# Hybrid gMLP and attention decoder step: two token tiles of v take the places of two gate tiles between the last attention blocks

## The chip, the cores and the metric

The kernel runs on one core of one Trainium2 chip. The metric is the device time of one execution in microseconds. The core's engines are TensorE (PE, with its weight loads listed apart as PEld), VectorE (DVE), ScalarE (ACT), GpSimd (POOL) and SyncE (SP), whose queue issues nearly all DMAs.

## The reference

One post-norm decoder layer is applied to 512 prompt tokens and 64 sample tokens (8 requests of 8 tokens), with the same weights and a width of 1024. All is in float32:

```python
h = x @ w_in                      # columns: gMLP u | gMLP v | q | k | attention v | gate_A | gate_B
u  = gelu(h[..., O_U:O_V])
va = layer_norm(gelu(h[..., O_V:O_Q]), ln_v_g, ln_v_b)
g_a, g_b = sigmoid(gate_A columns), sigmoid(gate_B columns)
y_a = u * (tril(W_s) applied to va in chunks of 128 positions + b_s)
y_b = sliding-window attention with sinks (window 128, 16 heads, 4 key/value heads)
m   = (g_a * (y_a @ w_pa) + g_b * (y_b @ w_pb)) @ w_o
x   = layer_norm(ALPHA * x + m);  x = layer_norm(ALPHA * x + swiglu(x))
```

The outputs are the new x of both groups, the key and value windows, and the normalised v rows of the sample tokens.

## The kernel before

A float32 product is made from three products of the fast format: each operand is split into a rounded part (hi, written by ACT) and the remainder (lo, written by DVE); hi by hi, hi by lo and lo by hi are summed in PSUM. Weights come as a stream of units of 128 x 1024 numbers (`wall`), in the order in which `_weights` puts them: `fetch` (L120) loads a unit into one of three `raw` buffers, and `convert` (L130) splits it into one of four `hi` and four `lo` buffers. `unit` (L145) hands out the next unit and splits `ahead` further ones.

There are three ways to multiply. `fm` (L302) makes a column tile of 128 output columns for all 576 tokens: 48 matmuls of 288 columns, weights stationary. `tm` (L315) makes a token tile: 128 tokens by 512 output columns, tokens stationary, 24 matmuls of 512 columns for a prompt tile over the 8 parts of the contraction (16 for the sample tile). `pair` (L218) makes two column tiles at once by the seven-product scheme of Strassen and Winograd: 7 products of 12 matmuls of 288 columns. It needs sums of quarters of x (`XSums`, and a fourth sum written over X), sums of quarters of the weights (`weight_group`, L158, on DVE and POOL) and additions of the results on DVE.

The work around the change stands in this order:

- **Attention.** There are 16 blocks (4 key/value heads by 4 windows). Between the steps of a block TensorE makes one column tile of w_in, listed in `FILLS` (L71): q and k tiles still missing, the eight u tiles, and last, in blocks 14 and 15 (counted from 0), the gate tiles g0 and g1 of g_a.
- **v** (`gmlp`, L876). The first 512 columns of v (here v0) are made for five token tiles at once, four units after each other; beside it run the sample tokens' attention values and, for four chunks, the loads and sums of quarters of x (`input_loads`, `input_sum`: 2 DMAs, 2 operations of POOL, 5 of DVE and 3 of ACT a chunk). Then come gelu of u and the second 512 columns (v1): three token tiles one by one, the last two together. `evacuate` applies gelu, `norm_steps` the layer norm on DVE.
- **Gates** (`merge`, L1019). Seven pairs make the other 14 gate tiles. Spare work (the rest of the norms, the eight `spatial_gate` steps, splits of y_a) is dealt out at fixed spots of the pairs. In this stage the order is the program's; in the two stages before a planner orders each engine's instructions, save where `issue_after` binds one behind another.
- Then the products with w_pa, w_pb and w_o, and the feed-forward part, whose pairs have the same seven products.

In the profile the gate tiles of the attention are called psg, the u tiles psu, v's sums acc_v, a pair's three sums x, y and z (xg for the gates, xf for the feed-forward part), attention's values po, the transposes of the samples' probabilities pst, the chunks xr, their split sums XS1h and so on, and weights ghi/glo in pairs, hi/lo elsewhere.

Of the kernel before, what the change touches and what calls it, by code (L numbers as in the profile page):

```python
# [70 lines left out]
FILLS = [tuple(x) for x in "q3 u0 k1 q4 q5 u1 q6 q7 u2 u3 u4 u5 u6 u7 g0 g1".split()]  # L71
# [8 lines left out]
class Builder:  # L80
# [678 lines left out]
    def projections_and_attention(self):  # L759
# [6 lines left out]
        self.kt, self.qs, self.u, self.T = [], {}, [], []  # L766
# [25 lines left out]
        for i, (g, n) in enumerate(blocks):  # L792
# [18 lines left out]
            fill = self.column_tile(*fills[i], ahead=1 + before_last)  # L811
# [18 lines left out]

    def column_tile(self, kind, c, ahead=1):

        ps = self.PS(f"ps{kind}{c}")
        u = self.unit(KC, ahead=ahead)
        self.fm(ps, u, self.xact, ks=range(7))
        yield
        self.fm(ps, u, self.xact, ks=range(7, KC))
        yield
        if kind == "k":
            self.evac_k(ps, c)  # L840
        elif kind == "q":
            self.evac_q(ps, c)
        else:
            tiles = self.u if kind == "u" else self.T
            if c % 2 == 0:
                tiles.append(self.C([2, NT], F32, f"{kind}{c}"))
            self.copied = self.nc.scalar.copy(
                out=tiles[c // 2][:, c % 2].rearrange("p (b c) -> p b c", b=2), in_=ps[:, :, :HB])
# [27 lines left out]
    def gmlp(self):  # L876
# [26 lines left out]
        def tile(t, out, u, ks):  # L903
            for k in ks:
                wh, wl = u[k // 2]
                self.tm(out, (*self.xact(k), self.XS[:, k, :]), wh[:, k % 2], wl[:, k % 2], t, k == 0, k == KC - 1)

        def evacuate(t, acc, half):
            s = slice(512 * half, 512 * half + 512)
            if t < NB:  # L910
                nc.scalar.activation(out=v[t][:, s], in_=acc, func=AF.Gelu_apprx_tanh)
            else:
                low = self.SG(f"vlow{half}")
                nc.scalar.copy(out=low[:NS, :512], in_=acc[NS:])
                self.low_added = nc.vector.tensor_tensor(
                    out=low[:NS, :512], in0=acc[:NS], in1=low[:NS, :512], op=ALU.add)
                nc.scalar.activation(out=v[t][:NS, s], in_=low[:NS, :512], func=AF.Gelu_apprx_tanh)
# [4 lines left out]
        acc = self.accumulators("v0")  # L922
        for n in range(4):
            with self.tc.issue_after(self.copied.ins):
                u = {n: self.unit(2)}
            for t in range(NB + 1):
                tile(t, acc[t], u, (2 * n, 2 * n + 1))
            if n == 0:
                self.sample_rest()
            if n == 1:  # L930
                self.input_sums()
                for c in range(3):
                    self.input_sum(c)
                fourth = self.input_loads(3)
        for t in range(NB + 1):
            evacuate(t, acc[t], 0)
        with self.tc.issue_after(self.turned.ins):
            for t in self.u:
                nc.scalar.activation(out=t[:], in_=t[:], func=AF.Gelu_apprx_tanh)
        us = [self.unit(2, ahead=int(n < 3)) for n in range(4)]  # L940
        for t in range(3):
            acc = self.bank(f"acc_v1_{t}")
            tile(t, acc, us, range(KC))
            if t == 0:
                with self.tc.issue_after(self.last_split.ins):
                    self.input_sum(3, fourth)
# [72 lines left out]
    def merge(self):  # L1019
        nc = self.nc  # L1020
        for t in self.T:
            nc.scalar.activation(out=t[:], in_=t[:], func=AF.Sigmoid)
        left = self.left(self.X, (*self.XSums[:2], self.input_sum3(), self.XSums[2]))
        self.first_pair(self.low_added)
        T = [self.T[0][:, i] for i in range(2)]
        gB = []
# [20 lines left out]
        with self.tc.manual_schedule():  # L1047
            for i in range(7):
                if i in (3, 4):
# [361 lines left out]
def _weights(w_in, w_pa, w_pb, w_o, w_gate, w_up, w_down):  # L1411
# [22 lines left out]
    start = {"q": o_q, "k": o_k, "u": 0, "g": o_g}  # L1434
    for kind, c in FILLS:
        fm(col(start[kind], c))
    for i in range(2):
        tm(w_in[:, o_v + 512 * i : o_v + 512 * i + 512])
    for j in range(2, 16, 2):
# [85 lines left out]
```

## Time and profile before

| | us |
|---|---|
| median of 3 runs | 877.47 |
| lowest of them | 877.05 |
| profiled execution, own time | 876.51 |
| span of the profiled execution | 874.8 |
| PE busy in the span | 864.8 |
| DVE, ACT, POOL busy | 629.4, 405.5, 194.5 |

The span runs from the first to the last instruction; the execution's own time is 1.7 us longer. The third of the three runs took 1218.6 us and stands far from the other two. All stage times below are in us from the span's start.

### The profile page before, as it was taken

How to read it: one execution, taken by the hardware profiler on the slowest of the kernel's cores; microseconds unless marked ns; L12 is line 12 of the kernel's file. 1: busy time of each engine (PE TensorE's matmuls, PEld its weight loads, DVE VectorE, ACT ScalarE, POOL GpSimd, SP SyncE). 2: the span in 40 equal slices, each digit the busy share in tenths (PEclk: the TensorE clock that was granted, in tenths of full speed). 3: DMA queues.
4: the chain of work that ended last, by engine and by line, in shares of the span. 5: the costliest groups of instructions: out<-in, count | busy, mean ns of one | idle time of the engine just before them, and what ended most of it. 6: DMA issues, size and time to landing. Idle time of an engine off the chain costs nothing.

```text
span 874.8 us, 14728 instructions
## 1 busy us (share of the span) xinstructions
PE 864.8 (99%) x5907; PEld 816.8 (93%) x5907; DVE 629.4 (72%) x933; ACT 405.5 (46%) x770; POOL 194.5 (22%) x206
## 2 busy tenths in 40 slices
PE   9999999999999999999999999999999999999996
PEld 7999999988899999999888999999999998888885
DVE  5878897657898888767778767777777789124237
ACT  6566566575464464333423544444444557111110
POOL 2013324253242203133203122222222210000003
PEclk9999999999999999999999999999999999999999
DMA  8422124255123134324640032222222335222202
GB/s 304 156 100 62 61 73 148 61 175 163 47 100 102 63 121 142 118 98 157 217 144 0 13 101 91 92 93 91 90 90 95 95 105 188 94 75 95 73 1 108
DMA packets 31168, 91.85 MB, mean 105 GB/s; under 512 B 3963, under 2 KB 9244, under 8 KB 31068
## 3 DMA queue, kind: packets, MB, share of 16 engines
q1 hardware_dynamic: 30764, 88.64, 30.9%
q10 hardware_dynamic: 336, 2.28, 0.7%
q8 instruction: 46, 0.75, 0.4%
q14 instruction: 22, 0.18, 0.1%
HBM read 86.77 MB, written 6.10 MB: 106 GB/s over the span
## 4 chain that ended last, share of the span: by engine, by line
PE 94%; DVE 3%; ACT 1%; DMA 0%; issue 0%; POOL 0%; DVEq 0%; SPq 0%; POOLq 0%; ACTq 0%
PE d L300 16%; PE xf L300 15%; PE zf L300 7%; PE acc_v L300 6%; PE acc_o L300 6%; PE pspa L300 6%; PE xg L300 5%; PE psu L300 5%; PE yf L300 4%; PE psq L300 4%; PE ffn L300 3%; PE xp L300 3%; PE zg L300 3%; PE psav L300 2%; PE psg L300 1%; PE zp L300 1%
## 5 line engine op out<-in xcount | busy, mean ns | idle before, releaser
L118 DVE TENSOR_TENSOR lo<-raw,hi 128x1024 fp32r<-128x1024 f32 x70 | 87.5, 1255 | 94.0 <-ACT hi L117 93.7
L118 DVE TENSOR_TENSOR glo<-raw,ghi 128x1024 fp32r<-128x1024 f32 (+1 forms) x93 | 100.5, 1087 | 53.6 <-ACT ghi L117 53.6
L300 PE MATMUL d<-hi,h 128*128 128x512 f32 (+1 forms) x440 | 128.0, 368 | 0.0
L117 ACT CAST hi<-raw 128x1024 fp32r<-128x1024 f32 x70 | 72.7, 1049 | 103.2 <-PE d L300 82.6
L117 ACT CAST ghi<-raw 128x1024 fp32r<-128x1024 f32 (+1 forms) x93 | 83.4, 900 | 58.7 <-DVE raw L180 56.9
L300 PEld LDWEIGHTS d<-hi,h 128*128 128x128 f32 x440 | 79.9, 189 | 13.8
L300 PE MATMUL d<-lo,h 128*128 128x512 f32 (+1 forms) x242 | 89.6, 370 | 0.0
L180 POOL TENSOR_TENSOR raw<-raw,t 128x512 f32<-128x512 f32 x31 | 41.0, 1323 | 193.3 <-DVE glo L118 164.1
L180 POOL TENSOR_TENSOR t<-raw,raw 128x512 f32<-128x512 f32 x31 | 43.0, 1387 | 111.9 <-DVE raw L180 111.9
L300 PE MATMUL xf<-x1T,ghi 128*128 128x288 f32 x320 | 64.9, 295 | 0.0
L118 DVE TENSOR_TENSOR glo<-t,ghi 128x1024 fp32r<-128x1024 f32 x31 | 63.0, 2032 | 1.9 <-ACT ghi L117 1.9
L300 PEld LDWEIGHTS d<-lo,h 128*128 128x128 f32 x242 | 45.6, 189 | 7.8
L300 PEld LDWEIGHTS xf<-x1T,ghi 128*128 128x128 f32 x320 | 51.3, 188 | 0.3 <-DVE u L231 0.2
L330 POOL TENSOR_SCALAR lnr<-lnmv 128x1 f32<-128x1 f32 (+1 forms) x15 | 12.3, 818 | 169.8 <-DVE lnmv L348 166.5
L645 POOL TENSOR_SCALAR_AFFINE_SELECT pc<-pt 128x512 fp32r<-128x512 f32 x24 | 23.1, 963 | 110.8 <-ACT pt L117 102.7
L300 PE MATMUL xf<-x1T,glo 128*128 128x288 f32 x160 | 47.1, 294 | 0.0
L300 PE MATMUL acc_o<-hi,m 128*128 128x512 f32 x144 | 46.4, 391 | 0.0
L621 ACT ACTIVATE work<-work,att 128x128 f32<-128x128 f32 x64 | 25.0, 392 | 42.1 <-DVE att L618 37.5
L300 PE MATMUL pspa<-yA,hi 128*128 128x288 f32 x256 | 44.3, 294 | 0.0
L300 PE MATMUL psu<-X,hi 128*128 128x288 f32 x256 | 44.1, 294 | 0.0
L300 PE MATMUL acc_v<-hi,X 128*128 128x512 f32 x128 | 41.8, 391 | 0.0
L300 PE MATMUL psq<-X,hi 128*128 128x288 f32 x224 | 38.8, 294 | 0.3 <-DVE kt L513 0.3
(370 smaller groups left out, 2472.6 us busy)
## 6 DMA issues: line engine op xcount, KB each, us to landing
raw<-in_wall_dram SPq DMA_DIRECT2D x132, 512.0 KB
open<-in_open_dram SPq DMA_DIRECT2D x7, 416.0 KB
xr<-in_xT_dram SPq DMA_DIRECT2D x8, 288.0 KB
z<-in_xtok_dram SPq DMA_DIRECT2D x4, 512.0 KB
out_y_prompt_dram<-z SPq DMA_DIRECT2D x3, 512.0 KB
circ<-bout SPq DMA_DIRECT2D x1, 1024.0 KB
Bsel<-circ SPq DMA_DIRECT2D x2, 512.0 KB
kc<-in_kcT_dram SPq DMA_DIRECT2D x2, 512.0 KB
```

The source lines that it names most:

```text
L117: self.nc.scalar.copy(out=hi, in_=src)
L118: return self.nc.vector.tensor_tensor(out=lo, in0=src, in1=hi.bitcast(F32), op=ALU.subtract)
L180: sub = lambda e, out, x, y: e.tensor_tensor(out=out, in0=x, in1=y, op=ALU.subtract)
L300: self.last_mm = self.nc.tensor.matmul(out, l, r, start=start, stop=stop, **more)
L330: self.nc.gpsimd.tensor_scalar_add(r[:n], mv[:n, 1:2], EPS)
L621: nc.scalar.activation(out=pr[:, r], in_=sel[:, r], func=AF.Exp, bias=nm[:, r : r + 1], accum_out=rs[:, r : r + 1])
L645: self.selected = nc.gpsimd.affine_select(out=f(out[:, i]), in_=f(pt[:, i].bitcast(F32)), pattern=[[0, 4], [sign, P]], compare_op=cmp, fil ...
```

## The change

`FILLS` ends with v0 and v1 in place of g0 and g1. These two name the first and second token tile of the first 512 columns of v, which `value_tile` makes in blocks 14 and 15, in the same two parts as a column tile (7/8 and 1/8 of the contraction). Its four units are asked for at the first of the two tiles and kept until the v stage. The sums are copied to SBUF raw; gelu follows after the attention. The v stage then makes the first 512 columns for three token tiles instead of five; the units of v1 are split one after each of the four steps there (`ahead=0`), the input chunks are dealt out one per step, the samples' attention values come after the second step, and gelu of u stands behind the gelu of v's sample tile. g0 and g1 become the first pair of the gate stage, which then has eight; the sigmoid of the two tiles at the head of `merge` goes, and the buffers of the pairs are renumbered. The weight stream has the same units in another order.

```diff
-FILLS = [... "q3 u0 k1 q4 q5 u1 q6 q7 u2 u3 u4 u5 u6 u7 g0 g1".split()]
+FILLS = [... "q3 u0 k1 q4 q5 u1 q6 q7 u2 u3 u4 u5 u6 u7 v0 v1".split()]
...
-            fill = self.column_tile(*fills[i], ahead=1 + before_last)
+            if fills[i][0] == "v":
+                fill = self.value_tile(fills[i][1])
+            else:
+                fill = self.column_tile(*fills[i], ahead=1 + before_last)
...
+    def value_part(self, t, out, us, ks):
+        for k in ks:
+            wh, wl = us[k // 2]
+            self.tm(out, (*self.xact(k), self.XS[:, k, :]), wh[:, k % 2], wl[:, k % 2], t, k == 0, k == KC - 1)
+
+    def value_tile(self, t):
+        ps = self.PS(f"psv{t}")
+        if t == 0:
+            self.v0w = [self.unit(2, ahead=int(n < 3)) for n in range(4)]
+            self.v0raw = self.C([2, 512], F32, "v0raw")
+        self.value_part(t, ps[:, 0], self.v0w, range(7))
+        yield
+        self.value_part(t, ps[:, 0], self.v0w, range(7, KC))
+        yield
+        self.copied = self.nc.scalar.copy(out=self.v0raw[:, t], in_=ps[:, 0])
...
-        acc = self.accumulators("v0")
+        acc = {t: self.bank(f"acc_v0_{t}") for t in (2, 3, NB)}
+        with self.tc.issue_after(self.turned.ins):
+            for t in range(2):
+                evacuate(t, self.v0raw[:, t], 0)
+        us = []
         for n in range(4):
-            with self.tc.issue_after(self.copied.ins):
-                u = {n: self.unit(2)}
-            for t in range(NB + 1):
-                tile(t, acc[t], u, (2 * n, 2 * n + 1))
+            for t in acc:
+                tile(t, acc[t], self.v0w, (2 * n, 2 * n + 1))
+            us.append(self.unit(2, ahead=0))
             if n == 0:
-                self.sample_rest()
-            if n == 1:
                 self.input_sums()
-                for c in range(3):
-                    self.input_sum(c)
-                fourth = self.input_loads(3)
-        for t in range(NB + 1):
+                chunk = self.input_loads(0)
+            else:
+                if n == 1:
+                    self.sample_rest()
+                self.input_sum(n - 1, chunk)
+                chunk = self.input_loads(n)
+        for t in acc:
             evacuate(t, acc[t], 0)
-        with self.tc.issue_after(self.turned.ins):
+        with self.tc.issue_after(self.gelu.ins):
             for t in self.u:
                 nc.scalar.activation(out=t[:], in_=t[:], func=AF.Gelu_apprx_tanh)
-        us = [self.unit(2, ahead=int(n < 3)) for n in range(4)]
...
-        for t in self.T:
-            nc.scalar.activation(out=t[:], in_=t[:], func=AF.Sigmoid)
...
-            for i in range(7):
-                if i in (3, 4):
+            for i in range(8):
+                if i in (4, 5):
                     g, u = (self.SG(f"gb{i}_{k}") for k in range(2))
...
-                (T if i < 3 else gB).extend((g, u))
-                if i == 6:
+                (T if i < 4 else gB).extend((g, u))
+                if i == 7:
                     self.spots = (0, 4, 5, 6)
-                gates(i, g, u, i < 6)
+                gates(i, g, u, i < 7)
...
-    for j in range(2, 16, 2):
+    for j in range(0, 16, 2):
         pair(col(o_g, j), col(o_g, j + 1))
```

## Rows read from the trace of the kernel before

**Rows 1.** The head of the profile page: busy time of each engine (share of the span, instructions), and the granted TensorE clock in 40 slices, in tenths.

```profile
PE 864.8 (99%) x5907; PEld 816.8 (93%) x5907; DVE 629.4 (72%) x933; ACT 405.5 (46%) x770; POOL 194.5 (22%) x206
PEclk9999999999999999999999999999999999999999
```

**Rows 2.** The waits of TensorE over the whole span: who waited for whom, us in total, times, longest.

```profile
PE warm L300 <- DVE ones L387: 1.2, 1, 1.2
PE ps L300 <- ACT hi L117: 0.8, 2, 0.4
PE psq L300 <- DVE kt L513: 0.3, 1, 0.3
PE pst L715 <- ACT g L847: 0.3, 1, 0.3
```

**Rows 3.** The chain that ended last, in order of time: start, us, what. The first row is a u tile between attention blocks, the second is v, and the last two are the second product (T1) of two pairs of the feed-forward part that follow each other.

```profile
160.08 6.33 PE psu L300 x48
194.87 44.67 PE acc_v L300 x196
...
514.27 1.60 PE zf L300 x12
...
525.43 1.60 PE zf L300 x12
```

**Rows 4.** Busy time by stretch: length, then busy us (and instructions) of PE, PEld, DVE, ACT and POOL, granted clock, DMA share, GB/s. The stretches are the last two attention blocks, v's first 512 columns, its second, the first gate pair, and the feed-forward pairs.

```profile
168.84:185.25 16.41, 16.12 (x124) 15.48 (x118) 7.34 (x15) 7.08 (x24) 5.85 (x9) 1.00 0.38 125
185.25:213.99 28.74, 28.74 (x187) 23.45 (x186) 18.83 (x33) 22.60 (x37) 12.31 (x9) 1.00 0.59 194
213.99:239.38 25.39, 25.39 (x114) 21.03 (x113) 21.68 (x30) 10.06 (x17) 7.76 (x7) 1.00 0.10 30
239.38:248.93 9.55, 9.55 (x73) 9.55 (x72) 8.99 (x13) 6.24 (x11) 5.75 (x6) 1.00 0.26 85
504.72:725.21 220.49, 220.47 (x1657) 220.06 (x1657) 168.07 (x208) 108.70 (x187) 49.13 (x38) 1.00 0.31 96
```

**Rows 5.** Timelines of ACT, DVE, POOL and PE around the last attention blocks: start, us, instruction, and in brackets the idle time before it with what ended it. The cast at 158.01 is the first step of the split of v's first unit.

```profile
158.01 1.05 ACT L117 CAST hi<-raw 128x1024 fp32r<-128x1024 f32 x1 [0.53 <-PE psu L300]
172.30 0.41 ACT L703 ACTIVATE samS<-samS,satt 128x136 f32<-128x136 f32 x1 [3.89 <-DVE satt L700]
...
175.77 0.17 DVE L706 TENSOR_TENSOR satt<-satt 128x8 f32<-128x8 f32 x1 [3.51 <-ACT satt L705]
...
179.66 1.22 POOL L645 TENSOR_SCALAR_AFFINE_SELECT pt<-pt 128x512 fp32r<-128x512 f32 x2
...
168.84 0.79 PE L300 MATMUL psg<-X,hi 128*128 128x288 f32 x4
182.57 0.62 PE L300 MATMUL po<-pt,av 128*128 128x512 f32 x2
184.70 0.66 PE L715 MATMUL pst<-ident,samS 128*128 128x128 f32 x4 [0.29 <-ACT g L847]
```

**Rows 6.** Timelines of DVE and PE from the start of v's second half into the second gate pair. The split at 216.33 is that of the last unit of v1; those at 236.17 and 237.31 are the first pair's; that at 250.95 is used by the second pair's matmuls at 253.70.

```profile
216.33 1.22 DVE L118 TENSOR_TENSOR lo<-raw,hi 128x1024 fp32r<-128x1024 f32 x1
236.17 1.22 DVE L118 TENSOR_TENSOR glo<-raw,ghi 128x1024 fp32r<-128x1024 f32 x1
237.31 1.22 DVE L118 TENSOR_TENSOR glo<-t,ghi 128x1024 fp32r<-128x1024 f32 x1
239.57 0.68 DVE L915 TENSOR_TENSOR vlow<-acc_v,vlow 64x512 f32<-64x512 f32 x1 [1.04 <-ACT vlow L914]
250.95 2.17 DVE L118 TENSOR_TENSOR glo<-t,ghi 128x1024 fp32r<-128x1024 f32 x1
...
239.38 0.42 PE L300 MATMUL xg<-X,ghi 128*128 128x288 f32 x2
253.70 0.30 PE L300 MATMUL xg<-XS2h,ghi 128*128 128x288 f32 x1
```

**Rows 7.** DVE and POOL beside each other in the v stage and the first gate pair (same columns): an input chunk's operation on POOL, two POOL operations on weights, and then the same DVE addition twice, at 188.94 and, beside the POOL operation of 216.49, at 217.47.

```profile
211.13 0.80 POOL L980 TENSOR_TENSOR s<-xr 128x288 f32<-128x288 f32 x1 [5.67 <-DMA xr<-in_xT_dram]
216.49 2.20 POOL L180 TENSOR_TENSOR t<-raw,raw 128x512 f32<-128x512 f32 x1 [3.73 <-DVE raw L180]
250.74 1.30 POOL L180 TENSOR_TENSOR raw<-raw,t 128x512 f32<-128x512 f32 x1 [2.66 <-DVE glo L118]
...
188.94 0.44 DVE L986 TENSOR_TENSOR xr<-xr,xr 128x288 f32<-128x288 f32 x1
217.47 1.54 DVE L986 TENSOR_TENSOR xr<-xr,xr 128x288 f32<-128x288 f32 x1
```

**Rows 8.** Waits of DVE and ACT between 185 and 240 for the input chunks, and of ACT over the whole span for a unit's load: us in total, times, longest.

```profile
DVE xr L986 <- POOL xr L979: 3.1, 2, 2.4
ACT XS1h L117 <- POOL xr L979: 4.6, 2, 3.0
...
ACT hi L117 <- DMA raw<-in_wall_dram: 9.5, 7, 4.7
```

More of the change, by code (lines that the diff above doesn't have):

```diff
@@ L67, in _bias_selector @@
     return sel
-FILLS = [tuple(x) for x in "q3 u0 k1 q4 q5 u1 q6 q7 u2 u3 u4 u5 u6 u7 g0 g1".split()]
+FILLS = [tuple(x) for x in "q3 u0 k1 q4 q5 u1 q6 q7 u2 u3 u4 u5 u6 u7 v0 v1".split()]
 FILLS = [(k, int(c)) for k, c in FILLS]
@@ L843, in column_tile @@
         else:
-            tiles = self.u if kind == "u" else self.T
             if c % 2 == 0:
-                tiles.append(self.C([2, NT], F32, f"{kind}{c}"))
-            self.copied = self.nc.scalar.copy(
-                out=tiles[c // 2][:, c % 2].rearrange("p (b c) -> p b c", b=2), in_=ps[:, :, :HB])
+                self.u.append(self.C([2, NT], F32, f"{kind}{c}"))
+            self.nc.scalar.copy(
+                out=self.u[c // 2][:, c % 2].rearrange("p (b c) -> p b c", b=2), in_=ps[:, :, :HB])
     def small_tables(self):
@@ L901, in gmlp @@
         rows = [P] * NB + [NS]
[L903 to L906, printed above, removed]
         def evacuate(t, acc, half):
@@ L916, in evacuate @@
                     out=low[:NS, :512], in0=acc[:NS], in1=low[:NS, :512], op=ALU.add)
-                nc.scalar.activation(out=v[t][:NS, s], in_=low[:NS, :512], func=AF.Gelu_apprx_tanh)
+                self.gelu = nc.scalar.activation(out=v[t][:NS, s], in_=low[:NS, :512], func=AF.Gelu_apprx_tanh)
             if half == 0 or t < 3:
@@ L945, in gmlp @@
                 with self.tc.issue_after(self.last_split.ins):
-                    self.input_sum(3, fourth)
+                    self.input_sum(3, chunk)
             evacuate(t, acc, 1)
@@ L1020, in merge @@
         nc = self.nc
-        for t in self.T:
-            nc.scalar.activation(out=t[:], in_=t[:], func=AF.Sigmoid)
         left = self.left(self.X, (*self.XSums[:2], self.input_sum3(), self.XSums[2]))
         self.first_pair(self.low_added)
-        T = [self.T[0][:, i] for i in range(2)]
-        gB = []
+        T, gB = [], []
         yA, yB = [], []
@@ L1433, in _weights @@
     fm(col(o_q, 2))
-    start = {"q": o_q, "k": o_k, "u": 0, "g": o_g}
+    start = {"q": o_q, "k": o_k, "u": 0}
     for kind, c in FILLS:
-        fm(col(start[kind], c))
+        if kind != "v":
+            fm(col(start[kind], c))
     for i in range(2):
         tm(w_in[:, o_v + 512 * i : o_v + 512 * i + 512])
-    for j in range(2, 16, 2):
+    for j in range(0, 16, 2):
         pair(col(o_g, j), col(o_g, j + 1))
```

3 lines of the change are left out of this document (2 added, 1 removed).

## The prediction, made before the changed kernel was run

> **What bounds the kernel now.** I read the head of the page first: TensorE is busy for 864.8 of 874.8 us, at the full granted clock in every slice, and the next engine, DVE, for 629.4 [rows 1]. A busy share can hide pauses, so I read TensorE's waits next. They are four kinds, 2.6 us in all, and one alone lies in the part that changes: 0.29 us before the samples' second transpose, at the end of the attention [rows 2, 5]. The stretches around the change say the same: TensorE fills v's two halves and the first pairs to the last hundredth [rows 4]. So here time is matmul time. An edit pays if TensorE gets fewer columns, and costs if another engine, freed of its cover, becomes late. The second question is therefore where DVE, ACT, POOL and the loads have slack, and it is read from the stretches and then from single instructions.
>
> **What TensorE gains.** Prices come from the chain, which gives the time from one group of matmuls to the next, not the overlapping durations of single ones.
> - Removed: two gate tiles by `fm`, 48 matmuls each. A u tile of the same form takes 6.33 us (131.9 ns a matmul) [rows 3], so 12.66 us.
> - Added: one pair, 84 matmuls. Two feed-forward pairs that follow each other reach the same product 525.43 - 514.27 = 11.16 us apart (132.9 ns a matmul) [rows 3], and TensorE has no pauses there that matter (0.02 of 220 us) [rows 4]. So 11.16 us.
> - Moved: two token tiles of 24 matmuls of 512 columns. 196 of these took 44.67 us, 227.9 ns each [rows 3], so 5.47 us a tile and 10.94 us together, out of the v stage into blocks 14 and 15. This is nothing by itself.
>
> The sum is 11.16 - 12.66 = -1.50 us. By stage it is larger and of both signs: the attention's end is 12.66 - 10.94 = 1.72 us shorter, v's first half 10.94 us shorter, the gates 11.16 us longer. The spare work of the gates (norms, spatial gates, splits) stays as it is and is spread over eight pairs instead of seven.
>
> **What hides the rest, and where the cover gets thin.**
>
> *Weights in blocks 14 and 15.* Tile v0 wants all four units of v within one block, where g0 wanted one. The planner already splits as early as a buffer comes free: at 158.01 ACT begins the split of v's first unit, the third after u7's, when u6's matmuls have let go of a buffer [rows 5]. In the new order that place belongs to v's third unit, the first two stand where g0 and g1 stood, and only the fourth waits for u7's buffer, free about 2.5 us before the tile starts. It is needed 18 matmuls into the tile, at 168.84 + 18 x 0.2279 = 172.94. The cast (1.05 us) and the subtraction (1.22) [rows 5, 6] fit: ACT stands idle for 3.89 us up to 172.30 and DVE for 3.51 us after 172.26 [rows 5]. If DVE does it only in that second gap it ends at 173.5, and TensorE loses 0.5 us. Bounds 0 and 0.5; I take 0, since the row at 158.01 shows the planner taking the first chance.
>
> *POOL's selections in block 15.* Less filling stands between the values of block 14 and those of block 15: 21 x 0.2279 = 4.79 us for 42 x 0.1319 = 5.54. The last selection ends at 180.88 and is used at 182.57 [rows 5], 1.69 us of slack, of which 0.94 stay. Cost 0.
>
> *The samples' transposes.* The wait of 0.29 us for the copy of the last tile stays, with a slightly smaller copy. Gain 0 to 0.29; I take 0.
>
> *ACT.* It loses the sigmoid of the two tiles and table loads that go with it, and is busy for 10.06 of 25.39 us in v's second half [rows 4], where gelu of u now goes. Nothing on the path: 0.
>
> *DVE in the v stage.* This is the term that matters. Before, DVE is busy 18.83 of 28.74 us in v's first half (65%) and 21.68 of 25.39 in its second (85%) [rows 4]. The first half shrinks to 28.74 - 10.94 = 17.80 us. Three splits leave it for the attention (3 x 1.22 = 3.66), so 15.17 us of work are left in 17.80. At the density of the first half 0.655 x 17.80 = 11.66 us of it get done, and 3.5 us run over; at the density of the second half all of it fits. The first half is the looser one because its work hangs on the input chunks, each a chain from load to POOL to DVE to ACT: DVE waits 3.1 us and ACT 4.6 us for POOL's part [rows 8]. Four such chunks now start one per step of 16 matmuls, 3.65 us.
>
> Late DVE work reaches TensorE in three places. The last unit of v1 takes a buffer that is let go when v's first half ends; its split ended at 217.55, and TensorE wants it 18 matmuls after 213.99, at 218.09: slack 0.54 us [rows 4, 6]. The first pair's weights are split by 237.39 for 239.38: 2.0 us [rows 6]. The second pair's end at 253.12 for 253.70: 0.58 us [rows 6], to which 1.04 us that DVE idled at 238.53 can be added. So what DVE is late by, less 0.54 us, is what TensorE loses at worst: 0 to 3.0 us. I take 1.0: the order on DVE is planned afresh, and the split that is needed first need not stand behind the late chunk, which leaves the later places with their 1.6 to 2.0 us.
>
> **The sum.** -1.50 + 1.0 = -0.5 us. The profiled execution took 876.51 us (span 874.8 and 1.7 around it), which gives 876.0. The median of the runs shown is 0.96 us above the profiled one; I put the forecast between the two and say 876.5.
>
> **Rivals.**
>
> *No stall at all.* DVE's work closes up as densely as in the second half. For it: that half already runs at 85% with the same kinds of work. Against: the chains of the chunks are not shortened by the change. 876.51 - 1.50 = 875.0, or 874.7 if the 0.29 us go too.
>
> *Late chunks and blocked DVE: slower than before.* DVE and POOL hold each other up where they run side by side: the same addition took 0.44 us at 188.94 and 1.54 beside the POOL operation that began at 216.49, and a split took 2.17 instead of 1.22 beside the one at 250.74 [rows 6, 7]. The four chunks bring eight POOL operations of 0.80 us [rows 7] into a stretch that is now short. If each blocked DVE for its whole length, that would be 6.4 us; half of it, 3.2, on the overrun of 3.5 makes DVE 6.7 us late, less 0.54 is 6.2 us at TensorE: 876.51 - 1.50 + 6.2 = 881.2. The point from which it is slower than before is a lateness of 0.54 + 1.50 = 2.04 us. Against it: much of DVE's work there is not for the next matmul, and DVE's idle time in the second half (3.7 us) takes some up. The Trainium skill, page "SBUF — State Buffer", section "SBUF: two separate sides", states a rule that speaks for this case: VectorE with two SBUF inputs and a GpSimd operation that reads SBUF share one port pair under an exclusive lock, and the later one blocks fully. By that rule the full 6.4 us would be the price; the trace agrees for the two collisions named, but most chunk operations in it lengthened nothing by so much, because DVE had other moments to work in.
>
> *The weights of tile v0 come late.* Four units in one block lean on loads that were spread over four. ACT waited up to 4.7 us for one load before [rows 8]. With that at the fourth unit: 876.51 - 1.50 + 1.0 + 4.7 = 880.7. Against: the load for v's fourth unit can start once the first is split, a whole block ahead.
>
> *The pair does not save what it should.* In the first gate pair DVE is busy 8.99 of 9.55 us [rows 4]; if the added pair ran as DVE lets it, not TensorE, it would cost up to 1.5 us more and eat the gain (876.5 to 878). Against: the added pair brings no spare work, and feed-forward pairs run with DVE at 168 of 220 us [rows 4]. It falls within the forecast's range and gets no chance of its own.
>
> **How the numbers follow.** Forecast (a stall of 0.3 to 2 us): 0.55. No stall: 0.20. Late chunks: 0.17. Late weights: 0.08. The range goes from the no-stall case with its 0.29 us and some tenths of scatter between runs (877.05 to 877.47 before), 874.3, up to the price of the late chunks, 881.0; what lies outside is the worst part of the last two cases and a little below. Two per cent of this kernel, about what a measurement can tell from no change, is 17.5 us. No case comes near it, on either side; I leave 0.01 for faster and 0.03 for a stall of a kind that I don't see.
>
> **What would show it.** In the changed profile: v's first half (from the last transposes to the first single token tile) about 17.8 us long; eight gate pairs, 11.16 us more between the first pair and the w_pa products; the tile psv in blocks 14 and 15 without a pause inside; TensorE's pauses, if any, at v1's seventh part (waiting for lo) or at the first two pairs (waiting for glo), of 1 us together. The prediction is wrong if TensorE waits inside the attention, if the pauses exceed 3 us, or if the w_pa products start later than before by more than 2 us with no pause of TensorE to show for it.

## The result and the profile after

The changed kernel took 878.41 us (median of 20 runs), the kernel before 877.09 (also a median of 20). The ratio is 1.0015, 95% interval 1.0008 to 1.0022: a small loss where a small gain was forecast, 1.3 us slower instead of about 0.5 faster. It is far under the 2 per cent that tell one kernel from another at a glance, but it is outside its own interval, and so there is something to explain. The profiled execution took 878.71 us. Single runs of 1218.6 us (before) and 1731.5 (the last experiment) stand far from the rest and are left in the medians; without its one the last experiment's median would be 875.82 instead of 875.94.

The head of the page says the same as [rows 1]: TensorE is busy for 99% of the span, at the full granted clock.

```profile
PE 865.3 (99%) x5895; PEld 815.9 (93%) x5895; DVE 631.3 (72%) x940; ACT 405.3 (46%) x775; POOL 191.8 (22%) x208
PEclk9999999999999999999999999999999999999999
```

The stretches that answer to [rows 4] (v's first half, its second, the first gate pair; length, then busy time and instructions of PE, PEld, DVE, ACT and POOL, granted clock, DMA) show where TensorE stops being full: 0.25 us in the first gate pair. v's halves have no pause; the first is 17.98 us long, where the prediction said about 17.8.

```profile
185.22:203.20 17.98, 17.98 (x140) 14.56 (x139) 12.82 (x25) 11.32 (x23) 5.00 (x7) 1.00 0.63 210
203.20:228.48 25.28, 25.28 (x114) 20.91 (x113) 20.26 (x33) 15.19 (x24) 8.00 (x10) 1.00 0.17 62
228.48:238.03 9.55, 9.30 (x70) 9.07 (x69) 8.05 (x13) 5.20 (x9) 4.31 (x4) 1.00 0.18 57
```

TensorE's waits, beside [rows 2], have two new lines, both before the product xg of a gate pair: 0.7 us for an addition (T) and 0.3 us for a split of weights (glo). The line of ps, 1.4 us for 0.8, lies in the opening of the kernel.

```profile
PE ps L300 <- ACT hi L117: 1.4, 2, 1.0
PE warm L300 <- DVE ones L387: 1.2, 1, 1.2
PE xg L300 <- DVE T L231: 0.7, 1, 0.7
PE psq L300 <- DVE kt L513: 0.3, 1, 0.3
PE xg L300 <- DVE glo L118: 0.3, 1, 0.3
PE pst L715 <- ACT v0raw L850: 0.2, 1, 0.2
```

The waits alone don't add up to the loss. So I also took, from TensorE's timeline of both kernels, the start of the first matmul of each stage, and set the distances side by side. That view also catches short stops that the list of waits doesn't count. All later experiments are read by the same table.

| from ... to ... | before | after | difference | by the prediction |
|---|---|---|---|---|
| samples' scores (pss) to the first matmul of v's stage | 17.54 | 16.21 | -1.33 | -1.72 |
| v's stage, to the first gate product (xg) | 54.13 | 43.26 | -10.87 | -10.94 |
| first gate product to the key outputs (in the second pair) | 19.11 | 20.02 | +0.91 | DVE's lateness |
| key outputs to the first w_pa product | 66.71 | 78.10 | +11.39 | +11.16 |
| w_pa products to the first product with w_pb (zp) | 34.94 | 35.79 | +0.85 | 0 |

The sum is +0.95 us, against the forecast's -0.50, and the stretches not shown differ by 0.06 at most, save the opening. The medians differ by 1.32. The losses against the matmul count are 0.39 + 0.07 in the attention and v, 0.91 + 0.23 in the first pairs, and 0.85 behind the last pair: 2.45 us. The opening took 19.55 and 19.98 us in two profiled executions of before and 19.63 to 20.84 in eleven of kernels with the change. It scatters from execution to execution; the means are 19.77 and 20.19, but two executions of before are too few to say whether the change adds some tenths there.

### The profile page after: what moved, and what is told of

Its sections match the earlier page's. It is cut to its first block, busy times and chain, and to the rows that moved or that the text cites. A ratio compares the mean times of both kernels' runs of the same rounds, so it can differ in the third digit from the quotient of the medians.

```text
span 877.0 us, 14725 instructions
## 1 busy us (share of the span) xinstructions
PE 865.3 (99%) x5895; PEld 815.9 (93%) x5895; DVE 631.3 (72%) x940; ACT 405.3 (46%) x775; POOL 191.8 (22%) x208
## 4 chain that ended last, share of the span: by engine, by line
PE 62%; DVE 0%; POOL 0%; DVEq 0%; issue 0%; POOLq 0%
PE d L300 16%; PE xf L300 15%; PE zf L300 7%; PE acc_o L300 6%; PE pspa L300 5%; PE yf L300 4%; PE ffn L300 3%; PE xp L300 3%; PE zp L300 1%; PE yp L300 1%; PE ffn L1235 0%; PE x1t L1235 0%; PE xg L300 0%; DVEq L1532 0%; POOL lnr L331 0%; DVE z L1419 0%
## 5 line engine op out<-in xcount | busy, mean ns | idle before, releaser
L118 DVE TENSOR_TENSOR lo<-raw,hi 128x1024 fp32r<-128x1024 f32 x68 | 85.0, 1256 | 96.4 <-ACT hi L117 96.0
L118 DVE TENSOR_TENSOR glo<-raw,ghi 128x1024 fp32r<-128x1024 f32 (+1 forms) x96 | 103.6, 1086 | 53.7 <-ACT ghi L117 53.7
L117 ACT CAST hi<-raw 128x1024 fp32r<-128x1024 f32 x68 | 70.5, 1048 | 104.5 <-PE d L300 82.6
L117 ACT CAST ghi<-raw 128x1024 fp32r<-128x1024 f32 (+1 forms) x96 | 86.0, 899 | 61.8 <-DVE raw L180 60.9
L118 DVE TENSOR_TENSOR glo<-t,ghi 128x1024 fp32r<-128x1024 f32 x32 | 65.3, 2039 | 1.7 <-ACT ghi L117 1.7
L300 PE MATMUL xg<-X,ghi 128*128 128x288 f32 x192 | 39.8, 300 | 0.7 <-DVE T L231 0.7
```

The source lines that it names most:

```text
L117: self.nc.scalar.copy(out=hi, in_=src)
L118: return self.nc.vector.tensor_tensor(out=lo, in0=src, in1=hi.bitcast(F32), op=ALU.subtract)
L300: self.last_mm = self.nc.tensor.matmul(out, l, r, start=start, stop=stop, **more)
```

## The experiments

**The changed kernel and the one before, once more.** One profiled run of each shows what repeats.

> The kernel before, once more, for its opening: how much the first matmul of the q tile (19.55 us after the start in the profile of before, 20.84 in that of after) moves from run to run with the landing of the first loads. If by 0.5 us or more, the 1.29 us between the two profiles at that place are the loads' and not the change's.

> The changed kernel, once more, for the same: its q tile starts anywhere between 19.5 and 21 us, while the later stretches repeat within 0.3 us (16.2, 43.3, 20.0 to 20.3, 35.8).

They took 877.06 and 877.9 us. Before gave 17.71, 54.14, 19.11, 66.71 and 34.88 us for the five stretches, after 16.19, 43.25, 20.52, 78.10 and 35.77. So four of the five repeat within 0.17 us; the first pairs of the changed kernel vary by half a microsecond from execution to execution.

**Block 15.** The prediction gave POOL's selections 0.94 us of slack after the change. In the changed kernel's trace they are late. The rows are one of DVE, two of ACT, then POOL and PE of block 15 in the order of time (start, us, instruction, idle time before it):

```profile
168.57 1.23 DVE L118 TENSOR_TENSOR lo<-raw,hi 128x1024 fp32r<-128x1024 f32 x1
...
174.16 0.41 ACT L703 ACTIVATE samS<-samS,satt 128x136 f32<-128x136 f32 x1 [3.98 <-DVE satt L700]
...
177.62 0.59 ACT L117 CAST pt<-pT 128x512 fp32r<-128x512 f32 x1
...
178.28 1.58 POOL L645 TENSOR_SCALAR_AFFINE_SELECT pc<-pt 128x512 fp32r<-128x512 f32 x1 [6.00 <-ACT pt L117]
179.91 0.95 POOL L919 MEMSET v<- 64x1024 f32 x1
180.94 0.64 POOL L645 TENSOR_SCALAR_AFFINE_SELECT pc<-pt 128x512 fp32r<-128x512 f32 x1
181.52 1.23 POOL L645 TENSOR_SCALAR_AFFINE_SELECT pt<-pt 128x512 fp32r<-128x512 f32 x2
...
182.32 0.98 PE L300 MATMUL po<-pt,av 128*128 128x512 f32 x2
```

The two matmuls that use the last selection take 0.98 us from 182.32, where two of this kind otherwise take 0.62 [rows 5]: TensorE stands for 0.37 us, to the end of the selections at 182.75. The list of waits has no line for it. Between the selections stands a MEMSET of 0.95 us that clears rows of v and is wanted much later. It is not new: it lay there before, covered by the 1.69 us of slack [rows 5]:

```profile
178.06 0.95 POOL L899 MEMSET v<- 64x1024 f32 x1
```

```diff
-        nc.gpsimd.memset(v[NB][NS:], 0.0)
+        with self.tc.issue_after(self.selected.ins):
+            nc.gpsimd.memset(v[NB][NS:], 0.0)
```

> The changed kernel with one edit: POOL's clearing of the sample tile of v (0.95 us) is bound behind block 15's last selection instead of standing between the first and the second. Theory (the shorter fills brought TensorE to the values of block 15 before POOL's selections were done): the stretch from the samples' score matmuls to the first matmul of the v stage goes from 16.21 us to about 15.85, and the pause inside the last po group (0.36 us) goes; the whole is 0.3 to 0.4 us faster than the changed kernel, a ratio to before of about 1.0011. Rival (the pause is TensorE's own, at the change from po to psv): nothing moves, 16.2 us and 1.0015.

Measured: 878.31 us, ratio 1.0013 (1.0004 to 1.0022), and 15.84 us for this stretch instead of 16.21. The selections now follow each other, and the pair of matmuls is back at 0.61 us:

```profile
179.72 0.64 POOL L645 TENSOR_SCALAR_AFFINE_SELECT pc<-pt 128x512 fp32r<-128x512 f32 x1 [0.18 <-DVE pt L118]
180.30 1.23 POOL L645 TENSOR_SCALAR_AFFINE_SELECT pt<-pt 128x512 fp32r<-128x512 f32 x2
181.59 0.95 POOL L920 MEMSET v<- 64x1024 f32 x1
...
182.02 0.61 PE L300 MATMUL po<-pt,av 128*128 128x512 f32 x2
```

The stretch is the clear evidence (-1.70 us against before, where -1.72 was counted); 0.37 us lies inside the interval of the total. It repeats: 15.83 to 15.85 us in the four kernels with this edit, 16.19 to 16.21 in the seven executions without it.

**The last gate pair.** In the changed kernel the addition that TensorE waits for 0.72 us stands on DVE behind splits of y_a and behind a split of w_pa's weights:

```profile
324.98 1.41 DVE L118 TENSOR_TENSOR yA<-u,yA 128x576 fp32r<-128x576 f32 x2
...
326.69 0.74 DVE L118 TENSOR_TENSOR yA<-u,yA 128x576 fp32r<-128x576 f32 x1
328.21 1.22 DVE L118 TENSOR_TENSOR lo<-raw,hi 128x1024 fp32r<-128x1024 f32 x1 [0.78 <-ACT hi L117]
329.35 0.45 DVE L231 TENSOR_TENSOR T<-xg,T 128x288 f32<-128x288 f32 x1
...
329.86 0.54 PE L300 MATMUL xg<-X,ghi 128*128 128x288 f32 x2 [0.72 <-DVE T L231]
```

Before, the same addition ended 0.19 us ahead of the matmul that uses it:

```profile
327.43 0.45 DVE L231 TENSOR_TENSOR T<-xg,T 128x288 f32<-128x288 f32 x1
...
328.07 0.43 PE L300 MATMUL xg<-X,ghi 128*128 128x288 f32 x2
```

Told from the first w_pa product, the addition now ends 0.52 us later (3.20 for 2.68), and the order of TensorE's matmuls has changed too: this last product xg stands behind 18 matmuls of w_pa instead of 21, 0.40 us earlier. The splits of y_a's last four parts come from `merge` after the pairs; the planner puts them among the last pair's additions. In the next kernel they are bound behind the last of these additions:

```diff
-        add(u, hi, x)
+        self.added = add(u, hi, x)
...
-        for g in range(len(yA), 8):
-            part(yA, self.u[g // 2][:, g % 2], self.C, f"yA{g}")
+        with self.tc.issue_after(self.added.ins):
+            for g in range(len(yA), 8):
+                part(yA, self.u[g // 2][:, g % 2], self.C, f"yA{g}")
```

(The expectation counts its stretch to the first xp matmul, which stands one product, 1.58 us, ahead of zp in the table.)

> The changed kernel with one edit: the splits of y_a's last four tiles on DVE are bound behind the last pair's last addition. Theory (in the eighth pair DVE does these splits first, the addition comes 1.9 us late and TensorE waits for it before the pair's last product): the 0.72 us wait of xg for DVE goes, and the stretch from the first w_pa matmul to the first matmul of the w_pb pairs goes from 34.2 us to about 33.4 as before the change; ratio to before about 1.0006. Rival (the wait only moves, to w_pa's matmuls that need the late splits): a new wait of pspa for DVE or ACT of 0.5 to 1 us, and 34 us or more.

Measured: 877.49 us, ratio 1.0005 (0.9996 to 1.0014), 34.94 us from w_pa to zp instead of 35.79, as before the change, and the wait is gone. DVE's addition still stands behind the split of weights, but that one now ends early enough:

```profile
326.74 1.23 DVE L118 TENSOR_TENSOR lo<-raw,hi 128x1024 fp32r<-128x1024 f32 x1 [1.45 <-ACT hi L117]
327.89 0.45 DVE L231 TENSOR_TENSOR T<-xg,T 128x288 f32<-128x288 f32 x1
...
328.39 0.54 PE L300 MATMUL xg<-X,ghi 128*128 128x288 f32 x2
```

So with these splits bound the 0.85 us are gone, at a place that the prediction had not looked at.

**The first pairs.** Here the changed kernel loses 0.9 to 1.4 us. The trace shows the fourth input chunk late: POOL begins with it at 211.44, when its load has landed, and ends at 214.01; DVE and ACT, with other work behind it, wait 2.43 and 4.72 us for it. Some 14 us later the first split of the first pair's weights ends at 229.10, after TensorE's first matmul of the pair at 228.48:

```profile
211.44 0.84 POOL L999 TENSOR_TENSOR s<-xr 128x288 f32<-128x288 f32 x1 [1.21 <-DMA xr<-in_xT_dram]
...
214.04 0.46 DVE L1005 TENSOR_TENSOR xr<-xr,xr 128x288 f32<-128x288 f32 x1 [2.43 <-POOL xr L998]
227.88 1.22 DVE L118 TENSOR_TENSOR glo<-raw,ghi 128x1024 fp32r<-128x1024 f32 x1
233.42 0.69 DVE L180 TENSOR_TENSOR t<-raw,raw 128x512 f32<-128x512 f32 x1 [1.46 <-DMA raw<-in_wall_dram]
...
214.04 0.43 ACT L117 CAST XS1h<-xr 128x288 fp32r<-128x288 f32 x1 [4.72 <-POOL xr L998]
...
229.15 0.40 PE L300 MATMUL xg<-X,glo 128*128 128x288 f32 x1 [0.25 <-DVE glo L118]
```

Two theories: DVE is late because it waits for the chunk, or because it has too much to do. The next kernel takes the wait away and leaves DVE's work: it leaves out the fourth chunk's two loads and two POOL operations, and DVE and ACT work on the third chunk's buffers once more. (In this expectation and the next, the "key transposes" are the product xg right behind the key outputs, 0.35 us after them: 20.37 us there is 20.02 in the table.)

```diff
-                chunk = self.input_loads(n)
+                if n < 3:
+                    chunk = self.input_loads(n)
...
-            self.split(hi[:, c], lo[:, c], self.s3raw[c])
+            self.split(hi[:, c], lo[:, c], self.s3raw[min(c, 2)])
```

> The changed kernel without the fourth input chunk's two loads and two POOL operations; DVE and ACT do the same eight operations on the third chunk's buffers once more, and the fourth sum's last quarter is split from the third's. So the work of DVE and ACT stays and only the waiting for load and POOL goes. Theory A (DVE is late at the first two pairs because it stood still for the fourth chunk, 2.4 us): the first pair's first split on DVE ends 1.5 to 2.5 us earlier against TensorE, the 0.3 us wait for glo goes, and the stretch from the first pair to the key transposes goes from 20.37 to about 19.5 us; 0.9 to 1.1 us faster, ratio to before about 1.0004. Theory B (DVE simply has too much work for the shortened stage, the standing still only fills slack): that stretch stays at 20.2 us or more and the ratio at 1.0013 to 1.0015.

Measured: 876.75 us, ratio 0.9996 (0.9988 to 1.0005), 19.11 us from the first product to the key outputs, exactly as before the change, and the third pair's short stop is gone too (77.87 for 78.10). The first split ends 1.87 us ahead of TensorE's first product instead of 0.62 behind it, and DVE even idles after it:

```profile
224.61 1.22 DVE L118 TENSOR_TENSOR glo<-raw,ghi 128x1024 fp32r<-128x1024 f32 x1
...
227.89 0.68 DVE L930 TENSOR_TENSOR vlow<-acc_v,vlow 64x512 f32<-64x512 f32 x1 [0.93 <-ACT vlow L929]
```

So it is the waiting, and not the amount of DVE's work. This kernel lacks the loads and POOL's operations as well, so by itself it does not tell the wait from them, and it does not yet say what a kernel that has the chunk can do about it.

**Work moved off the busy stretch.** The other way out would be to give DVE less: the norm of v's third token tile goes to the spare work of the pairs.

```diff
-            for step in norm(t):
-                step()
+            if t == 2:
+                n2 = norm(2)
+            else:
+                for step in norm(t):
+                    step()
...
-        self.todo = [..., n3[1], n3[2], n4[1], last]
+        self.todo = [..., n3[1], n3[2], n4[1], last,
+                     lambda: (n2[0](), n2[1]()), n2[2]]
```

> The changed kernel with one edit: the layer norm of v's third tile (two DVE operations of 1.28 us and the small ones) leaves the v stage and becomes spare work of pairs 2 and 3. Theory A and B alike: DVE reaches the first pair's splits about 2.9 us earlier, the load of the second pair's first weights starts earlier by as much, and the loss of 1.1 us in the first two pairs goes: 19.5 us from the first pair to the key transposes for 20.37; if nothing is given back later, ratio to before about 1.0003. Rival C (what is late in the first pairs is the load or ACT, not DVE's place in line): no change there. Given back would show in pairs 2 to 7, above all in the last, which now gets one more spare step: a larger wait there than 0.72 us.

Measured: 878.15 us, ratio 1.0013 (1.0004 to 1.0021). The wait for glo is gone, and a longer one has come, 1.85 us: 21.24 us for the first pairs, more than in the changed kernel. In the new order the sums of the second pair's weights stand on DVE ahead of the sample tile's addition (vlow). DVE waits for their load, ACT's gelu waits for vlow, the pair's copy stands behind the gelu, and TensorE waits for the copy:

```profile
230.12 0.69 DVE L180 TENSOR_TENSOR t<-raw,raw 128x512 f32<-128x512 f32 x1 [2.74 <-DMA raw<-in_wall_dram]
231.46 0.68 DVE L930 TENSOR_TENSOR vlow<-acc_v,vlow 64x512 f32<-64x512 f32 x1
...
232.17 0.63 ACT L932 ACTIVATE v<-vlow 64x512 f32<-64x512 f32 x1 [3.43 <-DVE vlow L930]
232.70 0.38 ACT L243 COPY T<-xg 128x288 f32<-128x288 f32 x1
...
233.13 0.40 PE L300 MATMUL xg<-XS2h,ghi 128*128 128x288 f32 x1 [1.85 <-ACT T L243]
```

This says nothing against the waiting; here less work on DVE ahead of the pairs did not help, because the order on it changed as well. That the last pair's loss is gone here as well (34.94) may come from the spare work falling on other spots, which I did not follow up.

**The chunk in a buffer of its own.** The fourth chunk's load waits for the third to let go of its buffers. Given others:

```diff
+        if c == 3:
+            t = self.C([2, NT], F32, "xr3")
+            p, q = t[:, 0], t[:, 1]
+        else:
+            p, q = self.SG(f"xr{c}"), self.SG(f"xr{c + 4}")
```

> The changed kernel with one edit: the fourth input chunk is loaded into a free large buffer instead of the two small ones that the third chunk lets go at about 207 us, so its loads are issued with the third's and its POOL work is done before DVE asks for it. Nothing is left out. Theory A (standing still for the fourth chunk is what makes DVE late at the first pairs): DVE waits less than 0.5 us for the chunk, the wait of xg for glo goes, and the stretch from the first pair to the key transposes is 19.1 to 19.4 us for 20.02 in the changed kernel (20.0 to 20.3 in its other variants), that between the second and third pair 11.6 for 11.82; 0.9 to 1.1 us faster than the changed kernel, ratio to before 1.0002 to 1.0006. Theory B (too much work on DVE): 20.0 or more, 1.0013.

Measured: 878.63 us, ratio 1.002 (1.001 to 1.0029), 20.57 us for the first pairs. The expectation was wrong: the chunk is early now, and there is no gain.

The same edit was also run together with the two before it, that of the MEMSET and that of y_a's splits:

> The changed kernel with three edits together: the clearing of v's sample tile behind block 15's last selection, the last four splits of y_a behind the last pair's last addition, and the large buffer for the fourth input chunk. If the three losses are all of it and don't give way to others, what is left of the change is the matmul time: 11.16 - 12.66 = -1.50 us in the stages against the kernel before (the stretches: block 15 and what surrounds it 15.84 for 17.54, v 43.27 for 54.13, gates 97.0 for 85.8, w_pa to w_pb 34.94 for 34.94), a ratio of 0.9981 to 0.9990 to before. If the pauses only move: 1.0000 or more.

Measured: 877.12 us, ratio 1.0002 (0.9993 to 1.0011). This is the second of the two cases expected: the first two losses are gone (15.85 and 34.94 us), the third stays: 20.90 us. The trace of the kernel with this edit alone says why. The wait has only changed its cause:

```profile
209.30 4.32 ACT L959 ACTIVATE u<-u 128x1152 f32<-128x1152 f32 x4
213.52 0.42 ACT L117 CAST XS4h<-xr 128x288 fp32r<-128x288 f32 x1
...
213.97 0.46 DVE L118 TENSOR_TENSOR XS4l<-xr,XS4h 128x288 fp32r<-128x288 f32 x1 [2.21 <-ACT XS4h L117]
227.17 1.22 DVE L118 TENSOR_TENSOR glo<-raw,ghi 128x1024 fp32r<-128x1024 f32 x1
```

The four gelus of u, which used to come after the chunk, now stand on ACT ahead of its last cast, and DVE waits 2.21 us for that instead of 2.43 for POOL.

**The gelus of u moved as well.** Two behind the gelu of v's second token tile, two behind that of the third, alone and with the three other edits.

```diff
+                self.v_gelu = nc.scalar.activation(out=v[t][:, s], in_=acc, func=AF.Gelu_apprx_tanh)
...
-        with self.tc.issue_after(self.gelu.ins):
-            for t in self.u:
-                nc.scalar.activation(out=t[:], in_=t[:], func=AF.Gelu_apprx_tanh)
...
+            if t > 0:
+                with self.tc.issue_after(self.v_gelu.ins):
+                    for x in self.u[2 * t - 2 : 2 * t]:
+                        nc.scalar.activation(out=x[:], in_=x[:], func=AF.Gelu_apprx_tanh)
```

> The changed kernel with the gelus of u moved alone, two behind the gelu of v's second token tile and two behind that of the third; the memset, the splits of yA and the fourth chunk stay as in the changed kernel. Theory: in the changed kernel the fourth chunk's casts stand ahead of the gelus, and VectorE waits for the chunk's load (2.43 us), so that the gelus hold up nothing but the third tile's gelu (0.35 us of VectorE's idle time). Moving them alone gains 0 to 0.4 us: 877.9 to 878.4 us, ratio 1.0010 to 1.0016, from the first product to the key outputs 19.7 to 20.2 us. Rival: if the gelus and not the chunk are what the first pairs lose by, 19.1 to 19.4 us here already, 877.3 us and a ratio of 1.0003.

Measured: 878.29 us, ratio 1.0014 (1.0005 to 1.0023), 20.00 us for the first pairs, as the theory said: alone the edit does nothing, since DVE still waits for the chunk (2.44 us).

> All three earlier edits (the memset behind the selections, the splits of yA behind the last pair's additions, the fourth chunk in buffers of its own), and the four gelus of u moved: two behind the gelu of v's second token tile, two behind that of the third, so that they no longer stand on ScalarE ahead of the fourth chunk's cast. Theory: the fourth edit of the set gained nothing because VectorE then waited 2.22 us (up to 213.78) for that cast, which stood behind 4.31 us of gelus. With the gelus out of the way that wait goes, the first split of the first pair's weights ends about 2 us earlier (from 228.2 to some 226.2) and the second pair's load starts as much earlier. From the first pair's first product to the key outputs 19.1 to 19.4 us (20.90 before this edit, 19.11 in the kernel before), the last pair and block 15 stay as they were mended (34.94, 15.84). 875.4 to 875.9 us, ratio 0.9983 to 0.9990. Rival: the first pairs' loss is the order on VectorE itself (the norms and the splits of the single tiles ahead of the weights' splits) or the second pair's load: then 20.3 to 20.9 us stay and the time is 876.8 to 877.2, ratio 1.000.

Measured: 876.61 us, ratio 0.9992 (0.9983 to 1.0001), 19.50 us for the first pairs. Of the 1.5 to 1.8 us that the theory wanted back in them 1.40 came; the total came out 0.7 us above its range, between the theory's and the rival's. DVE's 2.2 us wait is gone, but the first split moved less than foretold (it ends at 227.83 where 226.2 was expected; told from TensorE's first product, 0.08 us ahead for 0.58 behind), and DVE still idles for the second pair's load:

```profile
226.61 1.22 DVE L118 TENSOR_TENSOR glo<-raw,ghi 128x1024 fp32r<-128x1024 f32 x1
232.34 0.69 DVE L180 TENSOR_TENSOR t<-raw,raw 128x512 f32<-128x512 f32 x1 [1.65 <-DMA raw<-in_wall_dram]
```

**The last step of the norm behind the first split.** The second pair's load starts when the first split has let go of its buffer: in the kernel just shown the split ends at 227.83 and the load is issued at 227.96. So this split should not stand behind work that nobody waits for.

```diff
+            if x == "1":
+                self.first_glo = self.last_split
...
-            for step in norm(t):
+            steps = norm(t)
+            for step in steps[: 2 if t == 2 else 3]:
                 step()
+        self.last_step = steps[2]
...
         self.first_pair(self.low_added)
+        with self.tc.issue_after(self.first_glo.ins):
+            self.last_step()
```

> The run before last (all four edits with the gelus moved) with one more: the last step of the norm of v's third token tile, one VectorE operation of 1.28 us, is bound behind the first split of the first pair's weights instead of standing ahead of it. Theory: what is left of the first pairs' loss (0.39 us up to the key outputs, 0.24 us in the third pair) comes from the second pair's load, which starts only when that first split has let go of its buffer, so that VectorE idles 1.65 us for it at 230.7 to 232.3 and runs late from there on. With the split 1.3 to 2 us earlier that idle time falls under 0.5 us, and from the first product to the key outputs it takes 19.1 to 19.25 us (19.50 without the edit), from there to the w_pa products 77.87 to 77.95 (78.11). 875.9 to 876.3 us, ratio 0.9984 to 0.9992. Rival: VectorE simply has too much to do in the first two pairs, and the moved operation takes there what the load gives: 19.4 to 19.6 us and 78.1 stay, 876.6 us, ratio 0.9992.

Measured: 875.94 us, ratio 0.9989 (0.9980 to 0.9998): faster than the kernel before, with the interval just clear of 1. The first pairs take 19.12 us and the next stretch 77.86, as in the kernel without the fourth chunk's loads (19.11 and 77.87), so it was not the missing loads that helped there. The first split now ends at 225.09 and the load is issued at 225.16. DVE's idle time for the load is 0.18 us (its timeline), and TensorE's list of waits, below it, holds no line of a gate pair any more:

```profile
223.87 1.22 DVE L118 TENSOR_TENSOR glo<-raw,ghi 128x1024 fp32r<-128x1024 f32 x1
226.51 1.28 DVE L357 SCALAR_TENSOR_TENSOR v<-v,lnr,lnvb 128x1024 f32<-128x1024 f32 x1
229.78 1.79 DVE L180 TENSOR_TENSOR t<-raw,raw 128x512 f32<-128x512 f32 x1 [0.18 <-DMA raw<-in_wall_dram]
```

```profile
PE warm L302 <- DVE ones L389: 1.2, 1, 1.2
PE ps L302 <- ACT hi L117: 1.1, 2, 0.8
PE psq L302 <- DVE kt L515: 0.3, 1, 0.3
PE pst L717 <- ACT v0raw L852: 0.2, 1, 0.2
```

Against before the five stretches are now -1.71, -10.59, +0.01, +11.15 and -0.38 us: -1.52, where the matmul count said -1.50. That they agree so well is luck: two differences of another kind cancel. v's stage took 0.25 to 0.29 us more in all four kernels with the chunk in its own buffers than in the changed kernel (43.51 to 43.55 us; in the last one a split of v's weights ends at 206.31, and the matmul that uses it starts at 206.36, a little late). And the 0.38 us in the last stretch are no wait that was mended. In this kernel and the one before it the matmuls of w_pa behind the last pair follow each other faster, at the same granted clock of 1.00: 224 of them in 29.12 us, 130.0 ns each, where in before 219 took 28.89, 131.9 each. Why the pace differs is not shown. The medians differ by 0.97 us, not 1.52. The stretches are those of one execution: over the ten kernels with the change the difference of medians lies between 0.7 us below and 0.6 us above what the stretches give, so a single one of them is known no better than that.

## Why the prediction was wrong

The time lies inside the range, but the direction is wrong: the losses were 2.45 us where 1.0 was taken, and 1.50 is the point at which gain turns into loss. Two steps failed, those on POOL's selections and on the spare work; they are the third and fourth of the list.

- **What TensorE gains: right.** The eighth pair was priced at 11.16 us; the distance from the seventh pair's product y to the eighth's is 11.16. v's stage became 10.87 us shorter for 10.94. With the waits mended the sum is -1.52 for -1.50; without the two differences that cancel, 0.35 us more in v's stage than the price says and 0.38 less behind the last pair, it is -1.49. The rival that the added pair runs as DVE lets it didn't happen.
- **DVE in the v stage: right in size, and in place.** 1.0 us was taken, 0.91 + 0.23 = 1.14 came, at the first pairs as named (the first wait is the one for glo); in the second execution it was 1.64. The first split of the first pair's weights ended 2.0 us ahead of the first product before [rows 6] and is 0.62 us behind it now, so DVE was 2.6 us late where 3.5 was the worst estimate. The cause was given as the chain of the chunks, and the kernel without the fourth chunk's wait bears that out (19.11 us), and the last kernel, which has all the chunks, does too (19.12). At v's last unit, named as the tightest place, next to nothing was lost (0.07 us in all of v's stage).
- **POOL's selections: the step "of which 0.94 stay. Cost 0" failed.** It cost 0.37 us, inside the attention, where the prediction named a wait as what would prove it wrong. The step counted the shorter fill in block 15 alone. Told from the start of the samples' scores, TensorE wants the last selection 1.55 us earlier (14.86 us before, from 167.71 to 182.57, and 13.31 after, from 169.01 to 182.32): block 14's fill shrinks by about as much as block 15's, because there the value tiles also stand in place of gate tiles. And the selections end 0.57 us later (13.17 and 13.74): 0.35 us because ACT's cast stands behind the samples' exponentials, which came later when a split of v's weights pushed DVE's sums back, and 0.2 us because the first selection took 1.58 us instead of 1.38. 1.69 - 1.55 - 0.57 = -0.43 us, nearly the 0.37 us seen. The weights in these blocks, costed at 0, did not stop TensorE themselves, but their fourth split (at 168.57) is what pushed DVE's sums back. Moving the MEMSET was enough although both delays stayed: the selections then end 12.83 us after the scores' start, for a use at 13.32.
- **The last pair: the sentence "The spare work of the gates (norms, spatial gates, splits) stays as it is and is spread over eight pairs instead of seven" failed.** It treated a shift of the spare work as free and looked for late work only at three places in and after v's stage. The boundary to the w_pa products, where the planner takes over again, cost 0.85 us. In before the same addition stood behind the same sorts of splits and ended 0.19 us ahead of the matmul that uses it (327.43 + 0.45 for 328.07), so the slack there could have been read, and it was thinner than those that were. What used it up is read from the trace: the addition 0.52 us later, its product 0.40 earlier. That binding y_a's splits cures it is shown; that the shift of the spare work brought the new order about is argued, from this and from the loss being gone where the spare work lay otherwise. This is the largest missing term: with it alone the forecast would have been 877.4, no gain.
- **The samples' transposes and ACT.** The wait of 0.29 us became 0.24, for a cost taken as 0. ACT's gelus, also costed at 0, cost nothing in the changed kernel (moving them alone gave 20.00 us for 20.02), but only because the fourth chunk's casts stood ahead of them: with the chunk early they stood ahead of its last cast and held DVE for 2.2 us.
- **The rival of late chunks and blocked DVE** is the one that the result resembles, and only by half. The chunk was late, but DVE was not blocked by POOL's port use: the fourth chunk's operations took their usual 0.45 us. The Trainium skill, page "SBUF — State Buffer", section "SBUF: two separate sides", says that a VectorE operation with two SBUF inputs and a GpSimd operation that reads SBUF lock each other out. Such collisions occur in these runs: in the last kernel a DVE operation at 214.15 took 2.31 us instead of 1.28 beside one of POOL of 1.29, and the one at 229.78 took 1.79 instead of 0.69 beside one of 1.28; the first pairs still took 19.12 us there. What cost time was the order in the queues: an engine that stands at an instruction whose input is late also holds what is behind it.

What stays open: whether the change moves the opening by some tenths, why the w_pa matmuls go faster in two of the kernels, and why the first pairs of the changed kernel vary by 0.5 us between executions. Of that half microsecond 0.4 is one more stop of TensorE in the second execution, before the product xg at 235.95, which its list of waits does not hold either.

## What to carry to other kernels

Where one engine is full and the gain is a few matmuls, the time is decided by single instructions on other engines whose slack was just large enough; work out the new slack from a common origin for both sides (when the result is wanted, and when it is made), and do it at every boundary that the change passes, the far end of a lengthened stage included. Taking away one wait in a queue served in order may only bring up the next (chunk, then gelus, then a load behind a split), so the edits against it are worth something only together: here the first pairs took 20.57 us with the buffer alone, 20.00 with the gelus moved alone, and 19.12 with both, the norm's step and the two other edits.

## What the hardware showed that I had not expected

The list of waits misses short stops. The 0.37 us in block 15 stand in it nowhere; they show as a group of two matmuls that takes 0.98 us instead of 0.62 and in the distances between stages. Of the 2.45 us lost the list held 1.0 (0.7 and 0.3). Part of the rest is that a stop costs more than its wait: the two matmuls that start at 329.86, after the wait of 0.72 us, reach the next one in 0.38 us, the two at 330.37 in 0.27; so about 0.1 us comes on top. And the pace of TensorE is not the same in all kernels at the same granted clock: 130.0 ns or 131.9 for the same matmuls of w_pa.
